# A hybrid decoder layer on one core: TensorE in program order through the attention, row squares behind gates, pools by use, a small convolution on GpSimd

## The chip, the cores and the metric

One Trainium2 chip, one of its cores. TensorE multiplies, VectorE (DVE), ScalarE (ACT) and GpSimd (POOL) do the rest, SyncE (SP) and the other engines issue transfers. The metric is device time of one execution in microseconds; the median of three runs is what counts.

## What is computed

One layer, 4096 new positions of one prompt ("prompt") and 8 sequences of 8 tokens each ("sample", 64 tokens), width 1024, all in float32:

```python
h = rmsnorm(x, g_pre)
z = h @ w_in                                    # 1024 -> 2816 columns, in ten groups
cb, cc, ch, cg, q, k, v, ag, mq, mg = _split_cols(z)
u = cc * ch                                     # 256 channels
up = jnp.concatenate([conv_buf, u], axis=1)
conv = conv_w[0] * up[:, 0:t] + conv_w[1] * up[:, 1:t + 1] + conv_w[2] * up[:, 2:t + 2]
out_a = jax.nn.silu(cg) * cb * conv
out_b = jax.nn.silu(ag) * sliding_window_attention(q, k, v, sink)   # window 128, 8 heads, 2 kv heads, a sink logit per head
out_c = jax.nn.silu(mg) * cross_attention(mq, mem_k, mem_v)         # 4 heads, 256 memory tokens
y = jnp.concatenate([out_a, out_b, out_c], axis=-1) @ w_out
return x + rmsnorm(y, g_post), ...              # and the new convolution, key and value states
```

## The kernel before

**Input projection (0 to about 957 us).** Tokens go in eight blocks of 520 (64 sample tokens are the first 64 of block 0, two halves of 260 each). The product x @ w_in runs in three phases, each with a part of the columns (`PHASES`): half of the window queries, keys, values and the window's gates in phase 0, the convolution's columns in phase 1, the other queries, the memory's queries and gates in phase 2. Blocks 0 and 1 of phase 0 (`PLAIN_BLOCKS`) are multiplied plainly in eight products, all others in the seven products of a Strassen scheme. Each float32 operand is split into a high and a low part (`hi`, `lo` of x; `w[:, 0]`, `w[:, 1]` of the weights; ACT makes `hi`, DVE makes `lo`), and a product is three matmuls per pair (`product`, L351). In phase 0 every engine's order is the program's (`manual_schedule`), so a late instruction holds everything behind it on its engine; from phase 1 on the scheduler chooses the order by its own estimate of times, within the data dependences.

In the plain blocks, `plain_jobs` lists what each of the 16 steps does beside its products. `row` (`row_step`) takes one tile `nat` of 104 token rows and lets ACT sum its squares (L267); after five of them GpSimd raises the sums to -1/2 (L273, L274). `rows_diag` puts the factors on diagonals (L286; the trace calls this tile `mix_s`, whose buffer it shares), and `rows_product` multiplies them with ones, to spread them over the partitions (L292). `gains` and `scales` apply the norm's factors to x for block 2; `sums` make sums of weight tiles (L579 to L591, tiles `wa`); `done` is the gate stage of a finished block row: ACT's tanh `th` (L411), DVE's product (L412), a store to the scratch tensor `md` (L158). `plain_loads` issues the loads of each step.

**Phase 1, the convolution.** Per channel tile `ct` (two of them) and block, DVE multiplies two projected groups (`us` for the 64 sample tokens, L440; `ub` for the prompt, L445), runs three taps on each (L458, L460), multiplies with the gate (L461) and copies the sample's part to `mix_s` (L464). Sample tokens exist in block 0 only.

**Attention and output projection (about 957 us to the end).** `open_attention` opens the pools: one PSUM pool `ps` with the tags "z" (output products), "t" (transposes), "s" (scores), two buffers each, and "pv" (values). Sixteen chunks of 256 tokens each have window scores (`ws`, L1178), a softmax (copies L1180, L1181, maximum L1183, exponentials L1191), transposes (`wt`, L1201), values (`wo`, L1150 and L1156) with the gate product L1159, and a cross-attention (scores `xs` L1116, exponentials L1120, transposes `xt` L1131, their copies to `xpt`, DVE the first half and ACT the second, L1132, values `xo` L1033). `chunk_load` loads keys, `kst` and `vT`, and then queries, `q`; `load_mix` the gates `mix`. `values` transposes V (`vtp`, L1082, tag "t"; ACT copies it out at L1087). 33 blocks of 128 rows make the output: 48 matmuls `y` per block (L1404; two halves of 24), in between them `start()` begins a unit of the attention, so that TensorE has y products while a softmax runs:

```python
        pipe.start()
        if n == 0 and c < NCH:
            chunks[c].values(chunks[c - 1].vts[2])
```

A block ends with DVE's product with `gpost` (L1411), ACT's sum of squares (L1412), a power on GpSimd (L1418), DVE's residual `xr` (L1422) and the store. `gpost` is multiplied with sqrt(1024) once (L1435, GpSimd). In this whole stage the order is the scheduler's on all engines. Blocks 26 to 31 carry the sample's attention in stages (`smt`, `smot`, `svnt`, `sws`).

## Time and profile before

| | |
|---|---|
| median of three runs | 1596.27 us (1594.18 to 1598.16) |
| profiled execution | 1588.68 us, span 1587.0 us |
| mean granted TensorE clock | 0.996 |
| TensorE busy | 1555.9 us, 98% |
| DVE / ACT / POOL busy | 73% / 50% / 23% |
| moved | 305.65 MB, 193 GB/s |

A row of the waits reads: engine, the waiting instruction's tile and line, what it waited for; us in total, times, longest. A row of a timeline reads: start in us from the span's start, duration in us, engine, line, operation, output tile and input tiles, shape, how many alike; in brackets the idle time ahead of it and what ended it. Where a row of a timeline covers several instructions, the duration runs from the first's start to the last's end. Matmuls overlap: one starts before the previous one's end.

### The profile page before, as it was taken

To read this page: it belongs to the slowest core of one execution; us is meant where nothing else is said; L and a number is where in the kernel's file an instruction comes from. 1 tells how busy PE (TensorE), PEld (TensorE's weight loads), DVE (VectorE), ACT (ScalarE), POOL (GpSimd) and SP (SyncE) were. 2 spreads that over 40 slices of the span, in tenths; PEclk is the share of its full clock that TensorE was granted. 3 is DMA by queue.
4 is the path that set the end of the run, shared out by engine and by line. 5 is a ranking of instruction groups with operands and counts; after the bars stand their busy time and mean duration, and the time that the engine had idled before them with its cause. 6 is when DMAs were issued, how large, how long until landed. Compare 5 with 4: busy or idle time off the path is not lost.

```text
span 1587.0 us, 30080 instructions
## 1 busy us (share of the span) xinstructions
PE 1555.9 (98%) x11341; PEld 1408.1 (89%) x11341; DVE 1162.5 (73%) x2085; ACT 794.3 (50%) x2031; POOL 360.7 (23%) x590
## 2 busy tenths in 40 slices
PE   9979999999999999999999999999999999999998
PEld 9979999999999999999999997677777777777776
DVE  6759888898988777886777677666666666666643
ACT  6756666475222222344454355655555555555532
POOL 0212222211000000010002104544444444444210
PEclk9989999999999999999999999999999999999999
DMA  9969999878655333669666979977767667777332
GB/s 255 191 183 208 280 283 256 283 229 286 202 175 175 122 122 122 230 202 320 232 224 202 241 255 289 197 131 152 155 144 143 143 143 157 147 154 153 120 106 93
DMA packets 175110, 305.65 MB, mean 193 GB/s; under 512 B 31094, under 2 KB 104566, under 8 KB 174934
## 3 DMA queue, kind: packets, MB, share of 16 engines
q1 hardware_dynamic: 128069, 226.76, 45.8%
q0 software_dynamic: 46176, 75.92, 24.9%
q8 instruction: 90, 1.47, 0.4%
q10 hardware_dynamic: 720, 1.05, 0.2%
q14 instruction: 55, 0.44, 0.1%
HBM read 196.54 MB, written 108.12 MB: 192 GB/s over the span
## 4 chain that ended last, share of the span: by engine, by line
PE 81%; DVE 6%; DMA 5%; issue 4%; ACT 2%; POOL 1%; SPq 0%; ACTq 0%; DVEq 0%; POOLq 0%
PE c L351 42%; PE y L1404 22%; PE ws L1178 4%; PE xo L1033 2%; PE wo L1150 2%; PE wt L1201 2%; PE xt L1131 2%; PE xs L1116 2%; PE wo L1156 1%; DMA nat<-in_x_p 1%; DMA wr_2A<-in_w_in 1%; DMA x_0B<-in_xt 1%; PE mem_acc L760 1%; DVE z L358 1%; DMA vd<-v 0%
## 5 line engine op out<-in xcount | busy, mean ns | idle before, releaser
L1404 PE MATMUL y<-wo,mh 128*128 128x512 f32 (+1 forms) x1040 | 351.7, 400 | 0.0
L358 DVE TENSOR_TENSOR z<-c,z 128x520 f32<-128x520 f32 (+1 forms) x308 | 195.1, 646 | 96.0 <-PE c L351 95.0
L1404 PEld LDWEIGHTS y<-wo,mh 128*128 128x128 f32 x1040 | 194.3, 188 | 38.9 <-issue 2.4
L1404 PE MATMUL y<-wo,ml 128*128 128x512 f32 (+1 forms) x520 | 203.3, 391 | 0.0
L1191 ACT ACTIVATE sm<-sm,wnm 128x128 f32<-128x128 f32 x256 | 99.5, 391 | 52.6 <-DVE wnm L1185 52.4
L1125 POOL TENSOR_SCALAR xp<-xp,xrd 128x256 f32<-128x256 f32 x128 | 74.0, 584 | 225.2 <-DVE xrd L1121 222.0
L1404 PEld LDWEIGHTS y<-wo,ml 128*128 128x128 f32 x520 | 99.0, 190 | 15.9 <-issue 0.8
L1117 DVE TENSOR_REDUCE xmx<-xs 128x2 f32<-128x512 f32 x64 | 44.1, 689 | 57.6 <-PE xs L1116 57.4
L1178 PEld LDWEIGHTS ws<-kst,q 128*128 128x128 f32 x512 | 69.5, 190 | 12.8 <-issue 3.8
L1178 PE MATMUL ws<-kst,q 128*128 128x256 f32 x512 | 73.6, 285 | 5.4 <-issue 2.2
L1055 POOL DMA_DIRECT2D kst<-qd x64 | 38.7, 618 | 162.6 <-DVE wrd L1195 81.5
L1411 DVE TENSOR_TENSOR yn<-y,gpost 128x512 f32<-128x512 f32 (+1 forms) x66 | 45.1, 684 | 40.4 <-PE y L1404 39.4
L717 POOL CAST wmask<-negs 128x256 uint8<-128x256 f32 x1 | 1.5, 1461 | 321.9 <-DVE w_0S L177 321.9
L1412 ACT ACTIVATE y<-y 128x512 f32<-128x512 f32 (+1 forms) x66 | 38.5, 584 | 71.8 <-DVE yn L1411 71.8
L1203 ACT COPY wpt<-wt 128x512 f32<-128x512 f32 x64 | 37.1, 581 | 67.0 <-PE wt L1201 65.5
L1181 DVE COPY_PREDICATED sm<-wmask,ws 128x256 f32<-128x256 uint8 x124 | 52.2, 437 | 18.1 <-ACT sm L1180 18.0
L1211 POOL TENSOR_SCALAR_AFFINE_SELECT wpt<-wpt 128x512 f32<-128x512 f32 x64 | 52.0, 814 | 47.6 <-ACT wpt L1203 45.4
L1120 ACT ACTIVATE xp<-xs,xnm 128x256 f32<-128x256 f32 x128 | 58.9, 465 | 5.0 <-DVE xnm L1118 4.5
L1180 ACT COPY sm<-ws 128x256 f32<-128x256 f32 x128 | 45.1, 369 | 20.1 <-PE ws L1178 12.8
L1422 DVE SCALAR_TENSOR_TENSOR xr<-yn,yst,xr 128x1024 f32<-128x1024 f32 (+2 forms) x34 | 42.4, 1251 | 10.3 <-POOL yst L1418 10.3
L360 ACT COPY z<-c 128x520 f32<-128x520 f32 (+1 forms) x44 | 24.3, 553 | 50.7 <-PE c L351 47.9
L1066 POOL DMA_DIRECT2D q<-qd x64 | 42.7, 673 | 29.2 <-DMA x_1T<-hd_T 25.0
(956 smaller groups left out, 5132.0 us busy)
## 6 DMA issues: line engine op xcount, KB each, us to landing
q<-qd POOLq DMA_DIRECT2D x64, 384.0 KB, 7.8
xr<-in_x_p SPq DMA_DIRECT2D x32, 512.0 KB
nat<-in_x_p SPq DMA_DIRECT2D x39, 416.0 KB
o_yp<-xr SPq DMA_DIRECT2D x31, 512.0 KB
md<-th POOLq DMA_DIRECT2D x48, 260.0 KB, 6.4
qd<-zh SPq DMA_DIRECT2D x48, 260.0 KB
qd<-z SPq DMA_DIRECT2D x48, 260.0 KB
kst<-qd POOLq DMA_DIRECT2D x60, 192.0 KB, 4.8
```

The costliest lines, as they stand in the source:

```text
L351: TE.matmul(bank[:, :HW], l, r, start=first and i == 0, stop=last and i == 3 * KH - 1)
L358: add = lambda dst, other: V.tensor_tensor(dst, c, other, op=ALU.add)
L1117: V.tensor_reduce(mx[:, :nb], s, axis=AX.X, op=ALU.max)
L1120: S.activation(p[:, i, :], s[:, i, :], AF.Exp, bias=nm[:, i : i + 1], scale=SCALE, accum_out=den[:, i : i + 1])
L1125: G.tensor_scalar(p[:, i, :], p[:, i, :], rd[:, i : i + 1], 0.5, op0=ALU.mult, op1=ALU.mult)
L1178: TE.matmul(s3[:, hh, :], self.q[:, 4 + 2 * (2 * half + hh) + kvh, i * P : i * P + P], self.kst[:, 2 * kvh + part, i * P : i * P + 2 * P], ...
L1180: S.copy(sm[:, 2 * half : 2 * half + 2, :], s3[:, :, P : 2 * P])
L1181: V.copy_predicated(sm[:, 2 * half : 2 * half + 2, :], third["wmask"], third["negs"] if first else s3[:, :, 0:P])
L1191: S.activation(sm[:, hh, :], sm[:, hh, :], AF.Exp, bias=nm[:, hh : hh + 1], scale=SCALE, accum_out=den[:, hh : hh + 1])
L1211: G.affine_select(p3, p3, pattern=[[0, 4], [1, P]], compare_op=ALU.is_ge, fill=0.0, base=0, channel_multiplier=-1)
L1404: TE.matmul(acc, self.hl[l][:, k], wo[k][c0 // 512][:, r, c0 % 512 : c0 % 512 + c1 - c0], start=j == 0, stop=j == passes * KT - 1)
L1411: V.tensor_tensor(yn[:m, c0:c1], acc[:m], gpost[:m, c0:c1], op=ALU.mult)
```

## The change

Five things are changed; every engine's work is the same but for the named instructions.

- *Plain blocks.* In step (1, 2) the row square goes behind `done(0, 0)`; in (1, 0) two go ahead of `rows_product(0)`; in (1, 4) `rows_diag`, the gains for B11 and `rows_product(2)` go ahead of `sums(2, 1)`; the gains for B21 go to (1, 5); the loads of block 2's x for B11 and B21 go one step later.
- *Sample's convolution.* The product, taps, gate and `mix_s` for the 64 sample tokens go to GpSimd; the store to `md` covers the prompt's columns only.
- *Pools.* Each PSUM tag gets a pool of its own; `vp` moves, `mixp` joins the attention's pools, queries of even chunks get a pool `bq`, `xpt` has two buffers.
- *Loads and scale.* Chunk 2 loads its queries ahead of its keys; the scaling of `gpost` is dropped, the sum of squares is taken of y / sqrt(1024) instead.
- *TensorE's order.* From the first output product to the last, TensorE executes in the order in which the program issues. The other engines' orders stay the scheduler's.

```diff
@@ -437,7 +437,7 @@
         if ns:
             us = us_of[ct]
             V.memset(ub[:, 0:2], 0.0)
-            V.tensor_tensor(us[:, :, 2:10], zc[:, :ns].rearrange("p (b t) -> p b t", b=NB),
+            G.tensor_tensor(us[:, :, 2:10], zc[:, :ns].rearrange("p (b t) -> p b t", b=NB),
                             zh[:, :ns].rearrange("p (b t) -> p b t", b=NB), op=ALU.mult)
             store(a["o_convs"][ct], us[:, :, 8:10])
         else:
@@ -448,20 +448,22 @@
         if b == NBLK - 1:
             store(a["o_convp"][ct], ub_prev[ct])
         acc = temp(f"cacc{b}_{ct}")[:, :n]
-        parts = [(ub, acc[:, ns:n], m, None)]
         if ns:
-            parts.append((us, acc[:, :ns].rearrange("p (b t) -> p b t", b=NB), 8, 1))
-        for u, dst, w, batched in parts:
-            for i in range(3):
-                src = u[:, :, i : i + w] if batched else u[:, i : i + w]
-                if i == 0:
-                    V.tensor_scalar(dst, src, convw[:, ct, 0:1], None, op0=ALU.mult)
-                else:
-                    V.scalar_tensor_tensor(dst, src, convw[:, ct, i : i + 1], dst, op0=ALU.mult, op1=ALU.add)
-        V.tensor_tensor(acc, acc, zg, op=ALU.mult)
-        store(md[ct, :, tokens(b)], acc)
+
+            dst, t = (x[:, :ns].rearrange("p (b t) -> p b t", b=NB) for x in (acc, zc))
+            G.tensor_scalar(dst, us[:, :, 0:8], convw[:, ct, 0:1], None, op0=ALU.mult)
+            for i in (1, 2):
+                G.tensor_scalar(t, us[:, :, i : i + 8], convw[:, ct, i : i + 1], None, op0=ALU.mult)
+                G.tensor_tensor(dst, dst, t, op=ALU.add)
+        for i in range(3):
+            if i == 0:
+                V.tensor_scalar(acc[:, ns:], ub[:, 0:m], convw[:, ct, 0:1], None, op0=ALU.mult)
+            else:
+                V.scalar_tensor_tensor(acc[:, ns:], ub[:, i : i + m], convw[:, ct, i : i + 1], acc[:, ns:], op0=ALU.mult, op1=ALU.add)
+        V.tensor_tensor(acc[:, ns:], acc[:, ns:], zg[:, ns:], op=ALU.mult)
         if ns:
-            V.tensor_copy(mix_s[:, ct, :], acc[:, :ns])
+            G.tensor_tensor(mix_s[:, ct, :], acc[:, :ns], zg[:, :ns], op=ALU.mult)
+        store(md[ct, :, 2 * HW * b + ns : 2 * HW * b + n], acc[:, ns:])
 
     def finish(ph, b, zz, second):
 
@@ -620,13 +622,13 @@
             (0, 5): lambda: [*sums(1, 0), *row, *sums(1, 1), *fills(1, "S2", "S3"), *row],
             (0, 6): lambda: [*parts(1, "B11"), *row, *fills(1, "S1", "S4"), *sums(3, 0), *row],
             (0, 7): lambda: [*row, *fills(3, "S2", "S3"), lambda: rows_diag()],
-            (1, 0): lambda: [*parts(1, "B21"), lambda: rows_product(0), *z_rows(0, 1), *row, *row],
+            (1, 0): lambda: [*parts(1, "B21"), *row, *row, lambda: rows_product(0), *z_rows(0, 1)],
             (1, 1): lambda: [*z_rows(0, 0), *done(0, 1), *row, *row],
-            (1, 2): lambda: [*parts(1, "B12"), *row, *done(0, 0), *fills(3, "S1")],
+            (1, 2): lambda: [*parts(1, "B12"), *done(0, 0), *fills(3, "S1"), *row],
             (1, 3): lambda: [*sums(2, 0), *row],
-            (1, 4): lambda: [*parts(1, "B22"), *gains(2, "B11", "B21"), *sums(2, 1), lambda: rows_diag(),
-                             lambda: rows_product(2), *fills(2, "S2"), *row],
-            (1, 5): lambda: [*fills(2, "S3", "S1", "S4"), *scales(2, "B11"), *row],
+            (1, 4): lambda: [*parts(1, "B22"), lambda: rows_diag(), *gains(2, "B11"), lambda: rows_product(2), *sums(2, 1),
+                             *fills(2, "S2"), *row],
+            (1, 5): lambda: [*fills(2, "S3", "S1", "S4"), *gains(2, "B21"), *scales(2, "B11"), *row],
             (1, 6): lambda: [*gains(2, "B12"), *scales(2, "B21", "B12"), *row],
             (1, 7): lambda: [lambda: h_split(0), *gains(2, "B22"), *scales(2, "B22"), lambda: t_sum(0, 2, "T1"), *row,
                              *z_rows(1, 1)],
@@ -641,7 +643,7 @@
         if (b, s) == (0, 1):
             first_w("A12")
         for nb, o in {(0, 1): [(0, "B12")], (0, 2): [(0, "B22")], (0, 3): [(1, "B11")], (0, 4): [(1, "B21")],
-                      (0, 6): [(1, "B12")], (0, 7): [(1, "B22")], (1, 1): [(2, "B11")], (1, 2): [(2, "B21")],
+                      (0, 6): [(1, "B12")], (0, 7): [(1, "B22")], (1, 2): [(2, "B11")], (1, 3): [(2, "B21")],
                       (1, 4): [(2, "B12")], (1, 5): [(2, "B22")]}.get((b, s), ()):
             x_of(0, nb, o)
         row_queue()
@@ -954,26 +956,28 @@
 
     def open_attention():
 
-        nonlocal ps, mixp, wp, xp, vp, bp, yp
+        nonlocal ps, mixp, wp, xp, vp, bp, bq, yp
         own.close()
         mem_stack.close()
         psa.close()
         pa.close()
-        ps = ctx.enter_context(tc.tile_pool(name="ps", bufs=1, space=bass.MemoryType.PSUM))
-
-        mixp = ctx.enter_context(tc.tile_pool(name="mixp", bufs=1))
+
+        ps = {tag: ctx.enter_context(tc.tile_pool(name=f"ps{tag}", bufs=1 if tag == "pv" else 2, space=bass.MemoryType.PSUM))
+              for tag in ("z", "t", "pv", "s")}
+        vp = ctx.enter_context(tc.tile_pool(name="vp", bufs=5, side="right"))
         yp = ctx.enter_context(tc.tile_pool(name="yp", bufs=2, side="right"))
-        vp = att.enter_context(tc.tile_pool(name="vp", bufs=5))
+        bq = att.enter_context(tc.tile_pool(name="bq", bufs=1))
         wp = att.enter_context(tc.tile_pool(name="wp", bufs=2))
         xp = att.enter_context(tc.tile_pool(name="xp", bufs=2))
         bp = att.enter_context(tc.tile_pool(name="bp", bufs=1))
+        mixp = att.enter_context(tc.tile_pool(name="mixp", bufs=1))
         late = att.enter_context(tc.tile_pool(name="late", bufs=1))
         third["neg"] = late.tile([P, 4, 192], F32, name="sneg")
         third["scol"] = late.tile([P, 2], F32, name="scol")
         DMA.dma_start(third["neg"], a["smask"])
         DMA.dma_start(third["scol"][:, 0:1], a["sinkcol"])
 
-    ps = mixp = wp = xp = vp = bp = yp = None
+    ps = mixp = wp = xp = vp = bp = bq = yp = None
     att = ctx.enter_context(ExitStack())
 
     def psum(tag, name):
@@ -981,8 +985,8 @@
             return third["ps"].tile([P, 512], F32, tag="m", name=name)
         if tag == "pv":
 
-            return ps.tile([P, 2, 512], F32, tag=tag, name=name, bufs=1)[:, 0]
-        return ps.tile([P, 512], F32, tag=tag, name=name, bufs=2)
+            return ps[tag].tile([P, 2, 512], F32, tag=tag, name=name)[:, 0]
+        return ps[tag].tile([P, 512], F32, tag=tag, name=name)
 
     def work(pool, shape, tag, name, **kw):
 
@@ -1040,8 +1044,8 @@
             self.t0 = NS + CT * c
             self.ts = slice(self.t0, self.t0 + CT)
 
-        def pool(self):
-            return third["pre"] if self.c == 0 or self.c % 2 else bp
+        def pool(self, q=False):
+            return third["pre"] if self.c == 0 or self.c % 2 else bq if q else bp
 
         def load_keys(self):
             c, t0 = self.c, self.t0
@@ -1059,7 +1063,7 @@
 
         def load_queries(self):
 
-            self.q = self.pool().tile([P, 12, CT], F32R, tag="q", name=f"q{self.c}")
+            self.q = self.pool(True).tile([P, 12, CT], F32R, tag="q", name=f"q{self.c}")
             for part in range(2):
                 for hh in range(2):
                     half = hh if part == 0 else 1 - hh
@@ -1124,7 +1128,7 @@
 
                 G.tensor_scalar(p[:, i, :], p[:, i, :], rd[:, i : i + 1], 0.5, op0=ALU.mult, op1=ALU.mult)
             yield 1
-            pt = work(xp, [P, 2, CT], "xpt", f"xpt{c}_{h}", bufs=3)
+            pt = work(xp, [P, 2, CT], "xpt", f"xpt{c}_{h}")
             for kt in range(2):
                 t = psum("t", f"xt{c}_{h}_{kt}")
                 for i in range(nb):
@@ -1141,7 +1145,7 @@
             steps = [[], []]
 
             def both_halves():
-                o = ps.tile([P, 2, 512], F32, tag="pv", name=f"wo{self.c}_{i}", bufs=1)[:, :, :256]
+                o = ps["pv"].tile([P, 2, 512], F32, tag="pv", name=f"wo{self.c}_{i}")[:, :, :256]
                 o = o.rearrange("p a (h q) -> p a h q", h=4)
                 for n in range(2):
                     for kvh in range(2):
@@ -1216,8 +1220,9 @@
     def chunk_load(c):
         if c < NCH:
             chunks[c] = Chunk(c)
-            chunks[c].load_keys()
-            chunks[c].load_queries()
+
+            chunks[c].load_queries() if c == 2 else chunks[c].load_keys()
+            chunks[c].load_keys() if c == 2 else chunks[c].load_queries()
 
 
     def transpose_to(dst, srcs, name):
@@ -1231,7 +1236,7 @@
     def sample_mem(bh):
 
         nb = NB // 2
-        big = (bp, third["pre"])[bh].tile([P, 12, CT], F32, tag="q", name=f"sq{bh}")
+        big = (bq, third["pre"])[bh].tile([P, 12, CT], F32, tag="q", name=f"sq{bh}")
         km, (p, on, pt) = big[:, 0:8].rearrange("p (a b) n -> p a b n", a=2), (big[:, i] for i in (8, 9, 10))
         qb = big[:, 11].rearrange("p (j b c) -> p j b c", j=2, b=nb)
         vm = (mixp, yp)[bh].tile([P, KT, CT], F32, tag="mix", name=f"svm{bh}", bufs=1).rearrange("p (a b) n -> p a b n", a=2)
@@ -1409,12 +1414,12 @@
                 end = last and p == 2
                 if not end:
                     V.tensor_tensor(yn[:m, c0:c1], acc[:m], gpost[:m, c0:c1], op=ALU.mult)
-                S.activation((psum("t", "sq") if end else acc)[:m, : c1 - c0], acc[:m], AF.Square, accum_out=st[:m, p : p + 1])
+                S.activation((psum("t", "sq") if end else acc)[:m, : c1 - c0], acc[:m], AF.Square, scale=float(D) ** -0.5, accum_out=st[:m, p : p + 1])
                 if last and p == 1:
                     V.tensor_tensor(st[:m, 0:1], st[:m, 0:1], st[:m, 1:2], op=ALU.add)
 
             p = len(parts) - 1
-            V.tensor_scalar(st[:m, 3:4], st[:m, 0:1], st[:m, p : p + 1], D * EPS, op0=ALU.add, op1=ALU.add)
+            V.tensor_scalar(st[:m, 3:4], st[:m, 0:1], st[:m, p : p + 1], EPS, op0=ALU.add, op1=ALU.add)
             G.tensor_tensor(st[:m, 3:4], st[:m, 3:4], mhalf[:m, 0:1], op=ALU.pow)
             if last:
                 V.tensor_tensor(yn[:m, 768:D], acc[:m], gpost[:m, 768:D], op=ALU.mult)
@@ -1432,7 +1437,6 @@
     blocks[1].load()
     gpost = wa.tile([P, 2, 512], F32, tag="w", name="gpost").rearrange("p a n -> p (a n)")
     DMA.dma_start(gpost, a["gpost"].partition_broadcast(P))
-    G.tensor_scalar(gpost, gpost, float(D) ** 0.5, None, op0=ALU.mult)
 
     units = [8]
 
@@ -1479,6 +1483,8 @@
             next(stage, None)
         quarter[0] += 1
 
+
+    in_order.enter_context(tc.manual_schedule(engines={mybir.EngineType.PE}))
     for i in range(31):
         run(i, late_start if i >= 26 else start, (0, 2, 4, 6) if i < 2 else (2, 6))
     for stage in stages:
@@ -1486,6 +1492,7 @@
             pass
     run(31, lambda: None)
     run(32, lambda: None)
+    in_order.close()
     att.close()
 
 
```

## The prediction

> **What bounds the kernel now.** I read the page's busy shares first.
>
> ```profile
> span 1587.0 us, 30080 instructions
> ...
> PE 1555.9 (98%) x11341; PEld 1408.1 (89%) x11341; DVE 1162.5 (73%) x2085; ACT 794.3 (50%) x2031; POOL 360.7 (23%) x590
> ```
>
> TensorE is the bound: 31 us of the span are left to it, so the edits together can win no more than that and what TensorE loses at a lower clock; none takes work off it. The change can win only the waits in that remainder, and can lose wherever it puts a new wait in TensorE's queue. So the second view is TensorE's waits, summed by who ended them.
>
> ```profile
> PE rows_y L292 <- DVE mix_s L286: 9.2, 1, 9.2
> PE ws L1178 <- issue: 2.2, 2, 2.1
> PE ws L1178 <- ACT xp L1120: 1.7, 1, 1.7
> PE c L351 <- DVE lo_1T L342: 1.6, 1, 1.6
> PE idle L682 <- POOL mhalf L67: 1.5, 1, 1.5
> PE ws L1178 <- DVE z L358: 1.5, 1, 1.5
> PE vtp L1082 <- ACT xpt L1132: 1.5, 2, 0.8
> ```
>
> One wait is large (the row products, phase 0), the others lie in phase 1's first block (lo_1T) and at the attention's start (ws). In the long attention stage behind it there is nothing but two waits of 0.8 us at vtp. So three places can win, and the attention's 580 us can only lose. The timelines of each place are the third view.
>
> **Row squares and rows_product(2): -8.6 us.** TensorE stood still for 9.19 us and then ran on at half clock:
>
> ```profile
> 92.36 2.08 PE L292 MATMUL rows_y<-mix_s,ones 104*128 104x260 f32 x4 [9.19 <-DVE mix_s L286]
> ```
>
> ```profile
> 85.77:96.00 10.23, 3.64 (x13) 3.29 (x14) 7.09 (x17) 2.36 (x6) 0.00 (x0) 0.50 0.51 147
> 83.20:85.70 2.50, 0.00 (x0) 0.00 (x0) 0.32 (x1) 2.50 (x8) 0.00 (x0) 1.00 1.07 379
> 988.00:993.00 5.00, 2.91 (x19) 1.70 (x17) 1.46 (x5) 1.96 (x9) 1.52 (x3) 1.00 1.29 300
> ```
>
> (These windows list PE, PEld, DVE, ACT and POOL busy, then the granted clock.) The clock was full in the first 2.5 us of the stall and half in the rest and in the first 3.64 us of work behind it, which at full clock would have taken 1.8. The place is thus worth 9.2 + 1.8 = 11.0 at most. What held it:
>
> ```profile
> 85.38 0.69 DVE L579 TENSOR_TENSOR wa2A<-w_2A 128x512 f32<-128x512 f32 x1 [3.91 <-DMA md<-th]
> ...
> 91.58 1.00 DVE L286 TENSOR_SCALAR mix_s<-ident,r 104x104 f32<-104x104 f32 x5
> ```
>
> ```profile
> 75.34 1.06 ACT L267 ACTIVATE nat<-nat 104x1024 f32<-104x1024 f32 x1 [4.54 <-DMA nat<-in_x_p]
> ...
> 80.62 1.07 ACT L267 ACTIVATE nat<-nat 104x1024 f32<-104x1024 f32 x1
> ```
>
> ```profile
> 79.72 0.54 POOL L158 DMA_DIRECT2D md<-th  x1 [0.29 <-DVE zs L414]
> ```
>
> The chain reads: a row square on ACT waits 4.54 us for its x rows; the gates' th stand behind it; so their stores go out as late as 79.72; the third weight operand's sums on DVE wait for a buffer that these stores read (85.38); mix_s, which rows_product(2) multiplies, stands behind the sums. The change puts the square of (1, 2) behind done(0, 0), issues the last x rows ahead of x(2, B11), and moves sums(2, 1) and gains B21 behind the product. Then th need not wait, and at most 2 sums with the four lo_1B stay ahead of mix_s. What is late next is the last square itself: it would run at about 80.6 as the second one here did, POOL's power and mix_s follow in 2 to 4 us, and the product can start between 83.2 (no stall) and 89. I take a stall of 2.4, short enough for the full clock by the window of 83.20: 9.2 - 2.4 + 1.8 = 8.6 won. Ends: 5 (stall of 6) and 11.
>
> **Sample's convolution on GpSimd: -1.6 us.** DVE is the bound of this block alone:
>
> ```profile
> 400.00:420.00 20.00, 18.16 (x147) 17.86 (x148) 20.00 (x39) 5.64 (x7) 0.00 (x0) 1.00 0.46 149
> ```
>
> ```profile
> 409.07 0.28 DVE L460 SCALAR_TENSOR_TENSOR cacc<-us,convw,cacc 128x64 f32<-128x64 f32 x1
> 409.27 0.68 DVE L460 SCALAR_TENSOR_TENSOR cacc<-ub,convw,cacc 128x456 f32<-128x456 f32 x1
> ```
>
> Per channel tile five small instructions leave DVE (a product, three taps, the mix_s copy). From the start of the tap quoted to the next one's it is 0.20; five of 0.1 to 0.2, and a gate product that is narrower by 64 of 520, are an estimated 0.85, so about 1.6 for the two tiles, the second of which stands in front of the lo_1T that TensorE waits for. The wait is 1.6, so it is gone or nearly so. GpSimd takes seven small instructions per tile, was idle in this stretch, and its results go only to mix_s, which the end of the kernel reads. Ends: 0 (DVE is slowed by GpSimd's traffic as much as it is relieved) and 2. The Trainium skill (GPSIMD Engine Reference, section 8, Key points) says that GpSimd shares its SBUF interfaces with VectorE and contends with instructions of two SBUF inputs, and most of DVE's here have two; by that rule the sum would take 0 for this part. No row shows both at work in this block.
>
> **The attention's start: 0 us.** Gone: the 1.5 (the score tile has a PSUM pool of its own and no longer waits for the projection's last evictions), the 2.1 of "issue" at 991.59 and perhaps the 1.7.
>
> ```profile
> 962.87 0.77 DVE L1181 COPY_PREDICATED sm<-wmask,ws 128x256 f32<-128x256 uint8 x2
> ```
>
> ```profile
> 971.53 2.87 POOL L1435 TENSOR_SCALAR gpost<-gpost 128x1024 f32<-128x1024 f32 x1
> ```
>
> ```profile
> 991.59 0.36 PE L1178 MATMUL ws<-kst,q 128*128 128x256 f32 x1 [2.09 <-issue]
> ```
>
> That 2.1 waited for chunk 2's queries, which GpSimd issued behind gpost's 2.87; the scaling goes and the queries go ahead of the keys. In return TensorE is held to the program's order. It gets to ws2_1 after six products of y0_0, at about 960, but the two score slots are read by the copies that end at 963.6, behind DVE's backlog: a stall of some 3.4 where the scheduler had put other products. wt2_0 then waits some 2.0 for its softmax, and the loads of mix1 and gpost stand later on SP's queue, with 0 to 6 behind xo1_0 and wt3_0. Against 5.3 gone stand 5.4 and 0 to 6 new; some 3 us of badly interleaved weight loads go too. Zero, with ends of -6 and +8.
>
> **The steady chunks: +24 us.** What moves is small: per chunk, TensorE's two transposes of V for the next chunk. Before:
>
> ```profile
> 1099.62 0.66 PE L1131 MATMUL xt<-ident,xp 128*128 128x128 f32 x4
> 1100.03 0.48 PE L1404 MATMUL y<-wo,mh 128*128 128x512 f32 x1
> ...
> 1103.22 1.12 PE L1178 MATMUL ws<-kst,q 128*128 128x256 f32 x8
> ```
>
> Between 1100.03 and 1103.22 lie twelve products of y with vtp_0 behind the seventh and vtp_1 behind the ninth. In the program's order both stand right behind the xt, ahead of all twelve. The "t" tag has two PSUM slots, the xt of this step hold both, and they come free when the xpt copies have read them:
>
> ```profile
> 1099.76 0.69 DVE L1159 TENSOR_TENSOR mix<-mix,wo 128x512 f32<-128x512 f32 x1
> 1100.36 1.28 DVE L1422 SCALAR_TENSOR_TENSOR xr<-yn,yst,xr 128x1024 f32<-128x1024 f32 x1
> 1101.56 0.16 DVE L1193 TENSOR_TENSOR wden<-wden,wes 128x4 f32<-128x4 f32 x1
> 1101.63 0.42 DVE L1132 COPY xpt<-xt 128x256 f32<-128x256 f32 x1
> ```
>
> ```profile
> 1101.38 0.35 ACT L1132 COPY xpt<-xt 128x256 f32<-128x256 f32 x1
> ```
>
> So vtp_0 waits until 1101.73 (ACT) and vtp_1 until 1102.05 (DVE), with nothing of TensorE's able to pass them. The order of DVE and ACT here is the same in both kernels. The twelve products and the two transposes (some 0.1 each) take 3.19, so the twelve take 3.0; with 0.05 for the release, ws starts at 1102.05 + 0.05 + 0.1 + 2.85 to 3.0 = 1105.05 to 1105.2 instead of 1103.22: 1.85 lost. It can't be caught up: the chain on DVE starts with L1159, which waits for the wo products just ahead of xt, so it moves along with TensorE. Chunks 3 to 13 have this pattern: 11 x 1.85 = 20.4. Chunk 2 has no L1422 in the chain and 14 waits longer:
>
> ```profile
> 1028.61 0.69 DVE L1159 TENSOR_TENSOR mix<-mix,wo 128x512 f32<-128x512 f32 x1 [0.69 <-PE wo L1156]
> 1029.21 0.42 DVE L1132 COPY xpt<-xt 128x256 f32<-128x256 f32 x1
> ```
>
> ```profile
> 1478.60 0.47 PE L1404 MATMUL y<-wo,mh 128*128 128x512 f32 x1
> ```
>
> ```profile
> 1481.25 0.42 DVE L1132 COPY xpt<-xt 128x256 f32<-128x256 f32 x1
> ```
>
> Chunk 2: 1.02 from L1159 to the copy's end instead of 2.29, so 1.85 - 1.27 = 0.6. Chunk 14: 1481.67 - 1478.60 = 3.07 instead of 2.02, so 2.9. Sum 23.9. Ends 19 (a fifth of it hidden in a way I don't see) and 27. The window of 988 to 993 has a stall of 2.1 at full clock, so waits of 2 us should leave the clock alone. The Trainium skill (TensorE: Matmul & The Clock Gate, HAM oscillation) puts the limit at idle gaps of about 3.4 us, which agrees with these windows.
>
> **The end and the rest: +1.5 us.** smt0 and smot0 now follow xt without products of y between, on the same two slots: two waits like chunk 2's, 0.6 to 0.8 each. Ends 0 and 4. The factor D^0.5 that moves from gpost into the Square's scale changes no instruction's length; pool sides and buffer counts (xpt 2 instead of 3) hold nothing up, since a chunk's xpt is read by xo before the next but one is written.
>
> **Sum:** -8.6 - 1.6 + 0 + 23.9 + 1.5 = +15.2 against the profiled 1588.7 (span 1587.0 and 1.7 around it): 1604. That execution is 7.6 below the median of the three runs, 1596.3, to which the forecast is to be compared: 1611.5.
>
> **Rivals.**
> (1) Faster: the vtp waits are small. If the copies came within 0.3 us of the last xt (DVE ahead of TensorE by the time it gets there, xr no longer in front), the thirteen stalls would be some 0.3 each, 4 in all, and the sum -8.6 - 1.6 + 4 + 1.5 = -4.7, 1591.6; with a good start of -6, 1586. It decides when fewer than 0.7 us per chunk are lost. For it: with TensorE delayed, DVE has more time. Against it: L1159 at 1099.76 starts when wo ends, whatever went before, and xr stands behind it. 0.15.
> (2) Slower still: the start breaks up. The 3.4 us stall at ws2_1 and the late loads drop the clock as at 85.77, and ten microseconds run at half clock: 5 more, with 6 for mix1 and gpost: 1622. Against: of the stalls shown only that of 9.2 dropped it. The limit of the Trainium skill's page on the clock gate (TensorE: Matmul & The Clock Gate, HAM oscillation) is just this 3.4. 0.15.
> (3) The row stall isn't removed but has another last arrival (the last row square or the buffer's store): stall 6 to 9 and half clock again, 1616 to 1620. For it: ACT, POOL and DVE all have new orders there, and the path is a chain of three loads. 0.15.
> (4) Between (1) and the forecast: half of the vtp waits, sum about +3, 1599. 0.07.
>
> **How the numbers follow.** The forecast itself has 0.48. Its unknowns (rows 3 either way, start 7, chunks 4, end 2) give about 9 either way, 1602 to 1621; (2) and (3) lie up to 1624, (4) at 1599. Range 1596 to 1624, which leaves out most of (1) and a little above. About 0.3% (4.8 us) is what a measurement of this kernel tells from no change: slower by more is the forecast, (2), (3) and part of (4), 0.79; within it the rest of (4) and of (1), 0.08; faster most of (1), 0.13.
>
> **What would show it.** Right: thirteen waits of about 2 us at vtp behind ACT's or DVE's xpt, some 25 in all in the waits, and no wait over 3 us at rows_y; DVE below 20.0 of 20 in phase 1's first block; a stall of 2 to 4 at ws right behind the first six y. Wrong: vtp waits under 10 us in all, or a rows_y wait of 6 or more with a clock of 0.50 behind it.

## The result and the profile after

The changed kernel takes 1618.42 us (median of four runs, 1608.66 to 1622.35) against 1595.22 for the kernel before beside it: ratio 1.0163, 95% interval 1.0131 to 1.0196, slower. Repeated beside the variants the ratio was 1.0142 (1.0113 to 1.0172). The forecast was slower, by 15.2 us, 1611.5; the time lies in the range. In the two profiled executions the difference is 31.7 us (span 1618.7 against 1587.0), and the account is taken from these two.

The page of the changed kernel first, and behind it the row of `y` from the page before:

```profile
span 1618.7 us, 30127 instructions
...
PE 1569.5 (97%) x11341; PEld 1423.1 (88%) x11341; DVE 1163.1 (72%) x2075; ACT 796.0 (49%) x2031; POOL 376.1 (23%) x603
...
L1409 PE MATMUL y<-wo,mh 128*128 128x512 f32 (+1 forms) x1040 | 362.5, 411 | 0.0
```

```profile
L1404 PE MATMUL y<-wo,mh 128*128 128x512 f32 (+1 forms) x1040 | 351.7, 400 | 0.0
```

The same 11341 matmuls keep TensorE busy 13.6 us longer than before: the mean y product takes 411 ns where it took 400. Something slowed the matmuls themselves, beside the waits. TensorE's waits:

```profile
PE vtp L1086 <- ACT xpt L1136: 18.9, 14, 2.4
PE ws L1182 <- issue: 8.1, 1, 8.1
PE wt L1205 <- ACT sm L1195: 1.8, 1, 1.8
PE idle L684 <- POOL mhalf L67: 1.5, 1, 1.5
PE wt L1205 <- DVE xrd L1125: 1.5, 1, 1.5
PE ws L1182 <- ACT xp L1124: 1.4, 1, 1.4
PE rows_y L292 <- DVE mix_s L286: 1.4, 1, 1.4
```

The forecast's pattern is there: rows_y fell from 9.2 to 1.4, the wait at lo_1T is gone, and vtp waits 18.9 us in fourteen places. (Lines of the changed file lie up to five further down: L1404 is L1409, L1132 is L1136.) The 8.1 at ws is larger than forecast. One chunk on TensorE's timeline, to be held against the rows of 1099.62 to 1103.22 before:

```profile
1099.44 0.66 PE L1135 MATMUL xt<-ident,xp 128*128 128x128 f32 x4
1101.60 0.66 PE L1086 MATMUL vtp<-ident,vT 128*128 128x128 f32 x2 [1.50 <-ACT xpt L1136]
1102.01 0.66 PE L1409 MATMUL y<-wo,mh 128*128 128x512 f32 x1
1102.47 0.63 PE L1409 MATMUL y<-wo,ml 128*128 128x512 f32 x1
```

and DVE's in the same place:

```profile
1099.58 0.69 DVE L1163 TENSOR_TENSOR mix<-mix,wo 128x512 f32<-128x512 f32 x1
1100.18 1.28 DVE L1427 SCALAR_TENSOR_TENSOR xr<-yn,yst,xr 128x1024 f32<-128x1024 f32 x1
1101.38 0.15 DVE L1197 TENSOR_TENSOR wden<-wden,wes 128x4 f32<-128x4 f32 x1
1101.45 0.42 DVE L1136 COPY xpt<-xt 128x256 f32<-128x256 f32 x1
```

The chain is the one that the forecast read, a stall of 1.50 us. But behind it a y product takes 0.63 us, where the kernel before has 0.39:

```profile
1101.04 0.39 PE L1404 MATMUL y<-wo,ml 128*128 128x512 f32 x1
```

The windows around it (PE, PEld, DVE, ACT, POOL busy, then the granted clock) show why:

```profile
1098.73:1102.14 3.41, 1.91 (x16) 0.98 (x16) 3.31 (x9) 2.18 (x11) 2.42 (x4) 1.00 0.96 287
1102.14:1105.56 3.42, 3.42 (x10) 2.65 (x10) 0.54 (x1) 0.38 (x2) 0.00 (x0) 0.50 1.95 229
1105.56:1108.97 3.41, 3.41 (x22) 3.03 (x21) 1.42 (x4) 1.12 (x3) 0.00 (x0) 1.00 1.54 279
```

For exactly 3.41 us the clock is half, then full again. Nine of the twelve chunks 3 to 14 have such a half window (a stretch of 3.41 us at half clock), each worth 3.41 / 2 = 1.71 us.

The difference in the start times of the same matmul in both traces is taken stage by stage (ws31_0 names the first matmul of that score tile, y3_0 that of block 3's first half). At the first output product the changed kernel is 10.7 us ahead (960.01 and 949.34); at y3_0 it is 3.6 ahead (1038.98 and 1035.39); behind chunk 14, at ws31_0, it is 30.7 late (1495.66 and 1526.35); at the end 31.7. So: -10.7, then +7.1 at the attention's start, +34.3 in the chunks, +1.0 at the end.

That is the sum of one execution. A second profile of the same kernel (after_again, below) gives -15.2, +7.7, +29.7 and +1.0, together 23.2. Nearly all of the difference in the first term arises in one place: at 225 to 232 us the first execution waits 1.0 for hi_5B and 1.2 for lo_5B, runs a half window behind that (228.33 to 231.74) and loses 4.3 against the kernel before; the second loses nothing there.

### The profile page after: what moved, and what is told of

Read it like the earlier page. It is cut to its first block, busy times and chain, and to the rows that moved or that the text cites. A ratio compares the mean times of both kernels' runs of the same rounds, so it can differ in the third digit from the quotient of the medians.

```text
span 1618.7 us, 30127 instructions
## 1 busy us (share of the span) xinstructions
PE 1569.5 (97%) x11341; PEld 1423.1 (88%) x11341; DVE 1163.1 (72%) x2075; ACT 796.0 (49%) x2031; POOL 376.1 (23%) x603
## 4 chain that ended last, share of the span: by engine, by line
PE 78%; DVE 7%; DMA 5%; ACT 4%; issue 4%; POOL 1%; SPq 0%; ACTq 0%; DVEq 0%; POOLq 0%
PE c L351 42%; PE y L1409 21%; PE ws L1182 3%; PE xo L1037 2%; PE wt L1205 2%; PE xs L1120 2%; PE xt L1135 2%; ACT sm L1195 1%; PE wo L1154 1%; DVE ml L1390 1%; ACT xp L1124 1%; PE mem_acc L762 1%; PE wo L1160 1%; DMA nat<-in_x_p 1%; ACT mh L1389 1%
## 5 line engine op out<-in xcount | busy, mean ns | idle before, releaser
L1409 PE MATMUL y<-wo,mh 128*128 128x512 f32 (+1 forms) x1040 | 362.5, 411 | 0.0
L1409 PEld LDWEIGHTS y<-wo,mh 128*128 128x128 f32 x1040 | 203.1, 196 | 41.7 <-issue 1.6
L1409 PE MATMUL y<-wo,ml 128*128 128x512 f32 (+1 forms) x520 | 207.9, 400 | 0.0
L1409 PEld LDWEIGHTS y<-wo,ml 128*128 128x128 f32 x520 | 102.1, 196 | 17.3
L1182 PEld LDWEIGHTS ws<-kst,q 128*128 128x128 f32 x512 | 70.4, 192 | 14.8 <-issue 8.5
L267 ACT ACTIVATE nat<-nat 104x1024 f32<-104x1024 f32 x40 | 42.2, 1056 | 16.9 <-DMA nat<-in_x_p 16.8
```

Source lines behind the costliest of these rows:

```text
L1182: TE.matmul(s3[:, hh, :], self.q[:, 4 + 2 * (2 * half + hh) + kvh, i * P : i * P + P], self.kst[:, 2 * kvh + part, i * P : i * P + 2 * P], ...
L1409: TE.matmul(acc, self.hl[l][:, k], wo[k][c0 // 512][:, r, c0 % 512 : c0 % 512 + c1 - c0], start=j == 0, stop=j == passes * KT - 1)
```

## The experiments

The theory (A): the chunks lose to two transposes that wait for PSUM slots, and through this to the clock; the rest of the change wins some 10 us. Rivals: program order as such loses (C), the pools or loads lose (B, D), the half clock is a matter of the work and not of the stall (E). F, G and H, on smaller parts, are told where they are tested. "vtp first" means that the transposes of V go ahead of the scores.

| kernel | ratio to before, 95% interval | span |
|---|---|---|
| before with only the program order (e_manual) | 1.022 (1.019 to 1.025) | 1617.7 |
| changed kernel, again (after_again) | 1.0142 (1.0113 to 1.0172) | 1610.1 |
| three y products ahead of vtp (e_v3) | 1.0041 (1.0025 to 1.0057) | 1595.3 |
| before with only GpSimd's convolution (e_conv) | 0.9989 (0.9977 to 1.0002) | 1582.1 |
| vtp in the scores' slots (e_vs) | 0.9968 (0.9952 to 0.9984) | 1579.2 |
| vtp first, queries late (e_qlate) | 0.9945 (0.9929 to 0.9960) | 1579.9 |
| vtp first (e_vfirst) | 0.9943 (0.9923 to 0.9962) | 1575.4 |
| vtp first, keys first (e_keys) | 0.9938 (0.9915 to 0.9962) | 1578.1 |
| before with only the plain blocks' edits (e_rows) | 0.9937 (0.9922 to 0.9952) | 1576.1 |
| sum of the winning parts (e_best) | 0.9933 (0.9910 to 0.9956) | 1573.3 |
| without the program order (e_sched) | 0.9931 (0.9913 to 0.9949) | 1574.9 |
| vtp first, program order from block 2 (e_combo) | 0.9913 (0.9890 to 0.9935) | 1574.9 |

**One edit taken away, one edit alone.** The changed kernel without its program order:

```diff
-    in_order.enter_context(tc.manual_schedule(engines={mybir.EngineType.PE}))
     for i in range(31):
...
-    in_order.close()
```

> The changed kernel without the one edit on TensorE's order: from the first output product on the scheduler chooses, all other edits stay. Theory A (the two transposes of V wait for PSUM slots, and each such stall in one 3.41 us window of the clock record costs another half window; the rest of the change wins): about 10.5 us faster than before, the gain that the changed kernel already has at its first output product, and no half clock behind the attention's start; span 1575 to 1580. Theory B (the pools, the later loads or GpSimd's new work cost time in the attention): 0 to 5 us faster than before or slower, and chunks longer than the 37.8 us of before.

and the kernel before with that edit and nothing else:

> The kernel before with the one edit on TensorE's order and nothing else. Theory A: the row stall of 9.2 and the waits of 1.6 stay, the chunks' stalls come: 25 to 40 us slower than before, with vtp waits of 18 to 22 us and half-clock windows behind most of them; so slower than the changed kernel by the 10.5 that the other edits win. Theory D (the stalls come from the new pools, xpt with two buffers or the later loads, not from the order): within 5 us of before.

Ratios 0.9931 and 1.022. The order alone costs 2.2% (35 us), the rest of the change wins 0.7% (11 us): A in both; B and D fall as causes of the loss in the chunks. The waits of the kernel before with the order alone:

```profile
PE vtp L1082 <- ACT xpt L1132: 17.9, 14, 1.5
PE rows_y L292 <- DVE mix_s L286: 8.5, 1, 8.5
PE wo L1150 <- POOL wpv L1208: 3.2, 1, 3.2
PE ws L1178 <- ACT xp L1120: 3.1, 2, 1.6
```

Half windows were expected behind most of these stalls; in this execution five of the twelve chunks have one.

**Is it the order, or the slot?** The order left as it is, another slot for the two transposes:

```diff
-                t = psum("t", f"vtp{self.c}_{i}")
+                t = psum("s" if self.c > 1 else "t", f"vtp{self.c}_{i}")
```

> The changed kernel, TensorE's order untouched, but the two transposes of V of chunks 2 to 15 write to a PSUM tile of the scores' tag instead of the transposes' tag. Theory A (the slot is what is waited for): the vtp waits fall from 18.9 us to under 3, the half-clock windows of the chunks go with them, 30 to 34 us faster than the changed kernel, span 1584 to 1589. Theory C (program order as such costs the time, by worse interleaving and later work on the other engines): under 10 us faster than the changed kernel, chunk length stays over 39.5 us.

Another place in the program's order, the slot left as it is:

```diff
-        pipe.start()
         if n == 0 and c < NCH:
             chunks[c].values(chunks[c - 1].vts[2])
+        pipe.start()
```

> The changed kernel, but in each chunk's first step the transposes of V are issued ahead of the step's scores instead of behind its xt transposes, with the same tag and slots; TensorE stays in the program's order. Theory A: the slots are long free there and ScalarE has some 2.4 us (scores and values) to empty them before xt: vtp waits under 3 us in all, chunks of 37.8 us, 30 to 34 us faster than the changed kernel. Theory C: under 10 us faster, as the order is still the program's.

Spans 1579.2 and 1575.4, that is 39.5 and 43.3 less than the changed kernel's first profile and 30.9 and 34.7 less than its second. vtp has left the list of waits, but for one of 1.3 in the first, and neither has a half window in the chunks. In the second, vtp runs straight into the scores:

```profile
1088.62 0.38 PE L1086 MATMUL vtp<-ident,vT 128*128 128x128 f32 x2
1088.76 0.48 PE L1182 MATMUL ws<-kst,q 128*128 128x256 f32 x2
```

C falls: with the slots free, TensorE in program order is even 3.3 us quicker through the chunks than in the scheduler's (2.7 behind the variant without the order at y6_0, 0.6 ahead of it at ws29_0).

**How much of it is the clock?** A stall made shorter, not removed:

```diff
                     if k in starts:
                         start()                  # leaves the transposes of V in late_values
+                    elif k - 1 in starts:
+                        while late_values:
+                            late_values.pop()()
...
```

> The changed kernel, but in each chunk's first step three of the twelve y products (0.7 us) go ahead of the two transposes of V. Theory A with the clock as a rule of windows (a window of 3.41 us with 1.5 us or more without a matmul is followed by one at half clock): the stall falls from 1.5 to about 0.8 us, under the limit, so it costs 0.8 to 1.0 per chunk and no half windows in the chunks; 20 to 25 us faster than the changed kernel, though only 0.7 us per chunk (8 in all) were taken off the stall. Theory E (the half clock comes from the chunk's work as such, or from the vtp behind xt, whatever the stall's length): 8 to 10 us faster, half windows stay.

```profile
PE vtp L1086 <- ACT xpt L1136: 8.8, 11, 0.8
```

```profile
1098.59 0.65 PE L1086 MATMUL vtp<-ident,vT 128*128 128x128 f32 x2 [0.80 <-ACT xpt L1136]
1099.00 0.48 PE L1412 MATMUL y<-wo,mh 128*128 128x512 f32 x1
1099.32 0.39 PE L1412 MATMUL y<-wo,ml 128*128 128x512 f32 x1
```

The waits fell by 10.1 us (18.9 to 8.8), the span by 23.4 (14.8 against the second profile), and y behind vtp takes 0.39 again: no half window in the chunks. So a stall of 1.5 with a half window behind it costs 3.4, and one of 0.8 costs about 1. E falls for this.

The same kernel once more, for the grid:

> The changed kernel once more, beside the variants. Theory A with the rule of windows: the stalls at vtp are the same (17 to 20 us in all), but which of them lie within one window of the clock depends on where the grid of windows falls, so the number of half windows in the chunks differs from the 9 of the first profile (anything from 0 to 12), and the time by 1.7 us for each; 20 to 35 us slower than before. Theory E (the half clock follows from the work): 9 again.

```profile
PE vtp L1086 <- ACT xpt L1136: 18.9, 14, 2.4
PE ws L1182 <- issue: 8.5, 1, 8.5
```

The same 18.9 us of waits, but six half windows in the chunks where there were nine, and 4.6 us less from y2_0 to y31_1 (1015.29 to 1599.30 against 1011.30 to 1590.74). Three windows of 1.71 are 5.1. The work was the same, so the number isn't set by the work. With e_manual there are three executions: the chunks 3 to 14 lose 34.3, 29.7 and 27.8 us with nine, six and five half windows, and when 1.71 is taken off for each window, 18.9, 19.5 and 19.2 are left. The four runs of the changed kernel fit too: the slowest (1622.35) has a mean clock of 0.986, the fastest (1608.66) 0.994.

**The winning parts alone.** First the plain blocks' edits on the kernel before:

> The kernel before with only the plain blocks' edits (row squares behind the gates, loads one step later, products ahead of sums). Prediction's step: 8 to 11 us faster than before, rows_y waits 1.4 instead of 9.2 and no half window behind it. Theory G (the gain is partly given back where the projection ends, by stores and loads that are no earlier): 8 to 11 us at the first output product, but 3 to 5 less at the end.

```profile
PE rows_y L292 <- DVE mix_s L286: 2.5, 1, 2.5
PE ws L1178 <- issue: 1.7, 1, 1.7
PE ws L1178 <- ACT xp L1120: 1.7, 1, 1.7
PE c L351 <- DVE lo_1T L342: 1.6, 1, 1.6
```

0.63% (0.48 to 0.78), 10.0 us; ahead by 9.8 at phase 1's first product and by 10.9 at y30: nothing is given back, G falls. Then the convolution on GpSimd:

> The kernel before with only the sample's convolution moved to GpSimd. Prediction's step: 1.6 us faster, the wait of 1.6 at lo_1T gone. If GpSimd slows DVE as the shared memory interface would have it: 0 to 1 us slower, DVE's taps of 456 columns longer than 0.68.

Its ratio is 0.11% under 1 with an interval that holds 1, so a gain of 1.6 us is neither shown nor excluded by the times. In the trace the step is right: lo_1T isn't among TensorE's waits any more, and TensorE is busy without a gap from 400 to 420. Across this block (the matmuls that the kernel before runs from 405 to 440) all eleven profiled executions with the convolution on GpSimd gain 2.0 us, and the two of other kernels without it (e_rows, e_manual) gain nothing:

```profile
400.00:420.00 20.00, 20.00 (x169) 20.00 (x168) 20.00 (x31) 4.29 (x5) 15.97 (x14) 1.00 0.90 183
```

**The attention's start.** Where do 7.1 us go? In the changed kernel:

```profile
959.04 2.04 PE L1182 MATMUL ws<-kst,q 128*128 128x256 f32 x8 [8.07 <-issue]
```

```profile
954.73 0.62 ACT L173 CAST wo<-wor 128x512 fp32r<-128x512 f32 x1 [2.00 <-DMA wor<-in_w_out]
```

```profile
944.06 2.64 POOL L1070 DMA_DIRECT2D q<-qd  x4 [65.28 <-DVE lo_7T L342]
```

ws2_1 waits for the score copies, these stand behind the split of w_out's last tiles on ACT and DVE, and their load, issued at 946.69, landed only about 954.7. Beside it ran chunk 2's queries, which a pool of their own had let start at 944. The clock is lost there too (its share is the number ahead of the last two):

```profile
950.00:960.00 10.00, 1.93 (x9) 1.44 (x8) 5.07 (x9) 3.00 (x7) 0.00 (x0) 0.77 1.14 361
960.00:970.00 10.00, 8.16 (x36) 6.94 (x35) 5.25 (x18) 5.70 (x26) 3.02 (x5) 0.72 0.99 294
```

The half clock lies at 955.37 to 962.20 and 965.61 to 969.03. TensorE works in 6.57 us of it, so some 3.3 us are lost to the clock. To test whether the queries' load delays w_out (H) or w_out is late by itself (F), the keys were put first again in the variant with vtp first:

> The variant with the transposes of V first, but chunk 2 loads its keys ahead of its queries again, as before. In the changed kernel the queries' load (1.5 MB in four, issued at 944) runs beside the last loads of w_out (issued at 946.7, used by ScalarE at 954.7), for which VectorE and behind it the score copies wait. Theory H (that load delays w_out): the stall at ws2_1 falls from 8.0 to 1.5 to 4 us, and a wait of 2 us comes back at ws4_0; 2 to 5 us faster than the variant with both. Theory F (w_out is late by its own issue or buffers, whatever else is loaded): stall of 7 to 8 as it was, and a wait at ws4_0 on top, 0 to 3 us slower.

Void: GpSimd issued the queries at 943.8 all the same, as the scheduler orders GpSimd's queue and the pool was free. The stall stayed (8.4). So the pool of the queries was undone, again in the variant with vtp first:

```diff
-            return third["pre"] if self.c == 0 or self.c % 2 else bq if q else bp
+            return third["pre"] if self.c == 0 or self.c % 2 else bp
...
```

> The variant with the transposes of V first, but the queries of even chunks are back in the pool they had before, so that chunk 2's queries can't be loaded until ScalarE has split the last of w_out. (In the variant with the keys first the queries were issued at 943.8 all the same, since their pool, not the program's order, sets it; so it told nothing on this.) Theory H (the early load of the queries delays the last of w_out): the stall at ws2_1 falls from 8.0 to 1.5 to 4 us, some of it comes back as a wait at ws4_0 of about 2; 2 to 6 us faster than the variant with both. Theory F (w_out is late by its own issue or buffers): the stall stays at 7 to 8 and ws4_0 waits too: 0 to 4 us slower.

```profile
956.95 2.04 PE L1182 MATMUL ws<-kst,q 128*128 128x256 f32 x8 [3.38 <-issue]
```

```profile
960.58 1.98 POOL L1070 DMA_DIRECT2D q<-qd  x3 [79.19 <-DMA qd<-z]
```

```profile
PE ws L1182 <- issue: 3.4, 1, 3.4
PE rows_y L292 <- DVE mix_s L286: 2.8, 1, 2.8
PE xt L1135 <- ACT xpt L1136: 2.3, 1, 2.3
PE wt L1205 <- issue: 1.8, 1, 1.8
PE wt L1205 <- DVE sm L1200: 1.7, 1, 1.7
```

With the queries at 960 the stall is 3.4, and w_out's tiles come 3.6 us after their issue instead of 8 (949.29 to ACT's split at 952.87). The same holds in all fourteen traces: from the issue of w_out's tile to this split it is 3.4 to 3.7 us in the six with late queries and 8.0 to 9.5 in the eight with early ones. H is right on the stall. But 2.3 come back at xt and 1.7 at wt, from ws2_0 to y4 only 1.4 of 4.6 us are kept, and the ratio (0.9945) is that of the variant with the early queries (0.9943). So the stall of 8 is shown to come from a load that lies in another's way, but the start's loss as a whole isn't: the order alone, with late queries, loses 4.6 between y0_0 and y3_0 (e_manual), and the other edits without the order lose 2.2 (e_sched), together 6.8 of the 7.1.

**A version that beats both.** Twice the parts were put together, first on the changed kernel:

> The changed kernel with the transposes of V ahead of the scores, and TensorE held to the program's order only from the third output block on, so that the scheduler chooses in the first two. Theory A: the start is as in the variant with the scheduler's order (no wait over 5.5 us, the stalls at wt go), the chunks as in the variant with the transposes first: 3 to 5 us faster than either of those two, some 15 us faster than before, span 1570 to 1572. Theory F (the start is bound by the loads of w_out and not by the order): within 2 us of those two.

then on the kernel before, with its pools and loads:

> The kernel before with the plain blocks' edits, the sample's convolution on GpSimd, the transposes of V ahead of the scores from chunk 2 on and TensorE in program order from the third output block on; its pools and loads are those of before. Theory A: gains add up, 10.3 + 1.6 + 3 in the chunks = 15 us faster than before, span 1571 to 1573, 2 to 3 us faster than all variants. Theory G (part is given back at the attention's start by loads and stores that come no earlier): 10 to 12 us faster than before.

Both beat the kernel before (0.9913 and 0.9933) and the changed one by about 2%. Their gains of 11 to 14 us can't be told from those of the simpler variants, as the intervals overlap. In the first a wait of 5.9 stays at ws, whatever the order in the first two blocks, which speaks for the loads; the further gain of 3 to 5 us that A expected didn't come. For the second, 15 us were expected, and 7.0 to 14.3 are measured, which leaves room for theory G's 10 to 12. In its trace it is 14.1 ahead of the kernel before at ws3_0 and 13.9 at y30; 4.9 are won from ws8 to ws30, but at 1007.63 a wait of 2.5 at wt, with two half windows (1007.58 to 1014.41), takes back 4.4:

```profile
PE wt L1203 <- DVE sm L1198: 2.5, 1, 2.5
```

## Why the prediction was right, and where its sizes were off

*Row squares, -8.6:* right. Alone the edit wins 10.0 (7.6 to 12.4), near the upper bound of 11.0, since the half clock behind the stall went with it, as priced. The residual wait was 1.4 instead of the 2.4 assumed, but that is one execution. In the eleven profiles with this edit the wait at rows_y lies between 0.2 and 4.3; four of them (2.5, 2.8, 3.9 and 4.3) still have half clock behind it, and another with 2.5 has none. So a stall of 2.4 isn't always "short enough for the full clock"; this is the step that failed in the chunks too.

*Convolution, -1.6:* right, at its upper end: the wait at lo_1T is gone and the block is 2.0 shorter in every trace with the edit, though the times alone don't resolve it. The sentence that would have made it 0, contention of GpSimd and VectorE, didn't hold for VectorE: its taps take 0.68 beside GpSimd's work as before.

*The attention's start, 0 (ends -6 and +8):* mis-sized. +7.1 was measured from y0_0 on; the 1.7 that ws2_0 won, and that the forecast had counted here as the 1.5, lie just ahead of that point, so in the forecast's terms it is about +5.3. The step that failed is "a stall of some 3.4": it took DVE's copies at their old time, and 8.07 was measured. The new query pool let a load start 30 us earlier, into w_out's last load; without this the stall is 3.38. The prediction had listed the early queries only as a gain. Its sum also had nothing for the half clock behind the stall, which took some 3.3.

*The steady chunks, +23.9:* the mechanism is shown (slot or place changed, the wait is gone), the size was off: +34.3 in the profile for the chunks 3 to 14 (the 0.6 of chunk 2 lies ahead of y3_0). The stall term was near, a little high: the nine chunks with a half window lost 3.3 to 3.6 each, and 3.4 - 1.71 = 1.7 instead of 1.85; the three without lost 1.2, 1.2 and, where 2.9 were forecast, 1.1. What was missing is the clock, 9 x 1.71 = 15.4. The step that failed is "waits of 2 us should leave the clock alone". It rested on one stall of 2.09 that had been followed by full clock, and the grid of the clock's windows (last section) cuts that stall into 0.80 and 1.29 us. The limit of 3.4 us that the Trainium skill (TensorE: Matmul & The Clock Gate, HAM oscillation) gives for an idle gap does not hold here: 1.50 was enough.

*The end, +1.5:* +1.0; smt, smot and svnt wait 0.5, 0.3 and 0.5.

Of the rivals, (1) and (4) are excluded by 18.9 us of vtp waits, (3) by the 1.4 at rows_y. Rival (2), the start breaking up with half clock, came true beside the forecast and not in its place: 10.24 us at half clock, as it said, but at a cost of some 3.3 instead of 5, as part of it fell on the stall itself. By medians the change costs 23 us and not 31.7, since the profiled execution of the kernel before lies 6.5 us below its median and that of the changed kernel 2.0 above. Of the 16.5 by which 31.7 exceeds the forecast's 15.2, the clock in the chunks makes 15.4 and the start 4.7 (5.3 with chunk 2's 0.6 in the forecast for it); the stall term was 4.4 too large (23.3 against 34.3 - 15.4 = 18.9); row squares and convolution with all that lies ahead of ws2_0 gave 8.9 instead of 10.2, and the end 0.5 less.

That the time lies in the range is luck in part, beside a mechanism that was right. The clock in the chunks, worth 15.4 in one execution and 10.2 in the other, stood nowhere in the sum; the stall term erred the other way, and the median lies 5.6 under the upper bound of 1624. The near agreement ahead of the attention is luck as well: the first execution won more than forecast there and lost 4.3 at 225 to 232 us to waits that the forecast didn't have.

## What to carry to other kernels

Program order on TensorE cost nothing in the chunks once no instruction stood where its slot couldn't be free yet. Before an order is fixed, look for each PSUM tile's last reader and put the next writer of that slot where this reader has long run; here two lines in another order are worth 2%. A short stall of TensorE must be priced with the clock of what runs behind it, and what counts is where in the clock's windows it falls. A buffer that lets a load start earlier can also let it start beside the load that someone waits for. And one profile of a kernel is one draw: here two of the same kernel differ by 8.6 us, through half windows and short waits.

## What the runs showed of the hardware

- The granted clock changes in steps of 3.413 us on a fixed grid (10.24 us are three). Thirteen of the fourteen traces were cut along that grid (the other has a half window only at its end), the first 15 and last 12 us left out, and the time in each window in which no matmul ran was summed. Of the windows at full clock, some 5800 had under 1.45 us without a matmul, and none of these was followed by a half window; of 52 with 1.45 to 1.95, 25 were; of 20 with more, all 20. So a stall of 1.5 us can halve the clock for 3.41 us, if it lies within one window, and one of 2 us that is cut by the grid need not. What decides between 1.45 and 1.95 stays open.
- Once hit, a loop can be hit again and again: a chunk with stall and half window is 41.2 us long (ws10 at 1096.47, ws12 at 1137.67, ws14 at 1178.78), nearly twelve windows (40.96), so the next stall falls almost on the same place of its window. In the first execution half windows start at 1061.18, 1102.14, 1143.11 and 1184.07, twelve windows apart each time, and then one chunk is spared.
- In the kernel with only GpSimd's convolution, GpSimd's operations on 64 columns took between 0.32 and 4.74 us beside a VectorE that was full (20.00 of 20), while VectorE's taps of 456 columns stayed at 0.68; of its products `ub`, 0.63 before, one took 0.75 and one 0.65. GpSimd's spans are rough, and why some are long isn't shown, but VectorE's taps didn't pay:

```profile
401.58 4.74 POOL L440 TENSOR_TENSOR us<-z,z 128x64 f32<-128x64 f32 x1
...
411.68 0.33 POOL L465 TENSOR_TENSOR mix_s<-cacc,z 128x64 f32<-128x64 f32 x1
```
